# Three more kinds of edit to a fp32r transformer block: output stage 10 of 16 groups by seven, second down block 16 of 22, up stage's side stream eight steps sooner

## The chip, the cores and the metric

The kernel runs on one core of one Trainium2 chip. The metric is the device time of one execution in microseconds (us). A profile of one execution shows what each engine did: TensorE (PE) multiplies, VectorE (DVE) adds and subtracts, ScalarE (ACT) casts and applies functions, SyncE (SP) issues nearly all DMAs, GpSimd (POOL) does little here.

## The reference, cut to what matters

One transformer block for 256 tokens of width 2048 in float32. Three attention branches are gated and merged, the output projection is added to the residual, and a feed-forward part with a depthwise convolution of width 3 follows. The change touches the two products with `w_out` (2048 x 2048) and `w_down` (5632 x 2048), and work that goes on beside the product with `w_up`.

```python
def reference(x, mem, ...):
    ...
    merged = (g[:, :, 0] * (o_fox @ w_br_fox[l])
              + g[:, :, 1] * (o_sb @ w_br_sb[l])
              + g[:, :, 2] * (o_mem @ w_br_mem[l]))
    x = x + merged @ w_out[l]

    h2 = rms_norm(x, g_ffn[l])
    u = causal_depthwise_conv(h2 @ w_up[l], conv_w[l], conv_b[l])
    u_gate, u_val = jnp.split(u, 2, axis=-1)
    x = x + (jax.nn.silu(u_gate) * u_val) @ w_down[l]
```

## The kernel before, in words

**Precision.** Weights arrive from DRAM as float32 tiles of 128 x 1024 (`raw_*`). ACT casts a tile to the matmul's type (`hi_*`), DVE subtracts the cast from the tile (`lo_*`, "split" in what follows), and one product is three matmuls: activation hi x weight hi, activation lo x weight hi, activation hi x weight lo (`three`, L328 to L330 in the profile). The hi tiles have four buffers and so have the lo tiles (SBUFS = 4); a cast or a split that wants a fifth waits until PE has used the oldest. Raw tiles have four buffers of their own and, in the later stages, two more in turn (`raw_tile`).

**Blocks and groups.** The output product and the down product are computed by `blocked` (L367), each in two blocks of 1024 output columns. A block goes through pairs of k tiles (256 rows of the weights). One pair is a group, and a letter of the block's plan says how it is computed:

- `e`, by eight: 2 k tiles x 2 token tiles x 2 column halves = 8 products, 24 matmuls of 128x128 by 128x512. Two raw tiles are loaded (1.05 MB), cast and split.
- `s`, by seven: the 2 x 2 block product with seven products instead of eight, 21 matmuls. It needs four sums of the weights' quarters (T1 to T4) and three sums of the activations' (FS2 to FS4, and FS1). In the output and down stages the weight sums are made long before, and kept in DRAM; the group then loads 1.05 MB of sums beside 0.79 MB of weights, 1.835 MB in all. DVE splits three tiles of 1024 columns and one of 512.
- `f`, no matmuls: `form` makes the activation sums of one further pair (`pair_sums`, L334 to L346: DVE adds, ACT casts, DVE splits) for the down stage.

The gate stage (`name == "g"`) has a third form, `seven_here`: no sums are kept, DVE makes the four sums there from the raw tiles, into two further tiles (L440 to L443).

**Making sums ahead.** `halves` is one queue of (stage, block, pair, half) for all groups by seven that want kept sums, the output stage's first. Streams take from it beside other stages: each takes a group, loads its weights into a staging tile (`pre_*`), makes three DVE adds in place (`sums_in`, L247 to L251) and stores the sums to DRAM (`kept_*`). The last stream runs in the up stage (L1143): it begins after DU steps of that stage and takes a group every eight steps. A step is a call of `tick`, one per raw tile of the up stage.

**What sets the order.** Tile schedules instructions onto each engine's queue by priorities that follow from the program's order, except for those wrapped in `in_order`, which keep the order in which they are written. `ordered[0]` says whether `three` wraps its matmuls so. On each queue instructions then run in that order, and one that waits holds those behind it.

**After the last group by seven** of a block, `gather` adds its four banks into the residual on DVE. At the block's end four (in the last block five) adds follow and the output is stored.

Of the kernel before, what the change touches and what calls it, by code (L numbers as in the profile page):

```python
# [35 lines left out]
BLOCKS = 14  # L36
GS = 3
PF = 6
DU = 22


@with_exitstack
def hybrid_block(
# [25 lines left out]
    nc = tc.nc  # L69
# [28 lines left out]
    def later(gen):  # L98
        waiting.append(gen)
# [103 lines left out]
    def k_tiles(name):  # L203
# [19 lines left out]

    o_plans = ("eessesse", "eessesse")
    g_plans = (("", "esesesee", "esesesee"), ("esesesee", "esesesee", "esesesee"))
    d_plans = (
        "efefefef" + "sef" * 4 + "ssefsfssfssee",
        "efefef" + "sss" + "esss" * 3 + "ssee",  # L230
    )
    T1, T3, T4, T2 = range(4)
    FS2, FS4, FS3, FS1 = range(4)
    in_order = tc.keep_in_program_order
    dram = ctx.enter_context(tc.tile_pool(name="dram", bufs=1, space=bass.MemoryType.DRAM))
    by_k = lambda w: w[0].rearrange("(k p) n -> p k n", p=P)
    sums_of = {}
    ordered = [False]
    halves = deque(
        (name, by_k(w), nb, pr, h)  # L240
        for name, w, plans in (("o", w_out, o_plans), ("d", w_down, d_plans))
        for nb, plan in enumerate(plans)
        for pr in range(plan.count("s"))
        for h in range(2)
    )

# [120 lines left out]
    def blocked(name, w, nb, n0, plan, pair, sums, raw_tile, t4_tile, gathered, ready=None, form=None, apart=None):  # L367
# [4 lines left out]
        ns = plan.count("s")  # L372

        def a_of(p, j, t):
            v = pair(p, j)
# [83 lines left out]
            three(Y[1], *f_of(p, FS2), T2w, first, last)  # L459
            go_on()  # L460

        by_seven = seven_here if name == "g" else seven
        ahead = {}
        s, e = 0, ns
        for i, c in enumerate(plan):
            if c == "s":
# [4 lines left out]
                by_seven(s, s == 0, s == ns - 1)  # L471
                s += 1
                if s == ns:
                    later(gathered(n0, Y))
            elif c == "f":
                form()
            else:
                eight(e, i == 0, i == len(plan) - 1)
# [130 lines left out]
    def block(name, dt=F32):  # L609
        return bp.tile([P, 1024], dt, tag="blk", name=name)  # L610
# [384 lines left out]

    def merged_sums():
        yield 1
        for p in range(o_plans[0].count("s")):
            ms[p] = block(f"ms_{p}", F32R).rearrange("p (f l q) -> p f l q", f=4, l=2)
            pair_sums(mT[p], block(f"mw_{p}"), [(ms[p], slice(0, 4))])  # L1000
            yield 3

    raw_g = lambda name: wp.tile([P, PIECE], F32, tag="raw", name=name)

# [113 lines left out]

    raw_o = lambda name: raw_tile(name, lambda name: gp.tile([P, PIECE], F32, tag="pre", bufs=1, name=name))
    t4_o = (junk, lambda name: block(name)[:, :512])  # L1120
    for nb, plan in enumerate(o_plans):
        X = blocked(
            "o", w_out, nb, nb * PIECE, plan, lambda p, j: mT[p][:, j], lambda p, f: ms[p][:, f], raw_o, t4_o[nb],
            lambda n0, Y: gather(n0, Y, block),
        )
        for n in range(2):
            for t in range(NT):
                o = xres[:, t, nb * PIECE + n * 512 : nb * PIECE + (n + 1) * 512]
                nc.vector.tensor_tensor(o, o, X[t][n], ALU.add)
            later(hidden_T(2 * nb + n))  # L1130
# [120 lines left out]
        return dn[0].tile(shape, dt, tag=tag, name=name)  # L1251

    ov = out[0].rearrange("(t p) d -> p t d", p=P)
    N0, N1 = (plan.count("s") for plan in d_plans)
    sf = xt_pool.tile([P, 28, 2, P], F32R, tag="xt", name="sf")
    sf_more, sf_rest = [], []
    assert N0 == 11
# [3 lines left out]
    def s_of(p, f):  # L1261


        if f == FS1:
            return a_blocks[:, 2 * p, :, 1]
        if p < 9:
            return sf[:, 3 * p + f]
        if p == 9:
            return sf_more[0][:, f] if f < 2 else sf_rest[2]
        if p == 10:  # L1270
            return sf[:, 27] if f == 0 else sf_rest[f - 1]
        return a_blocks[:, 2 * (p - N0 + N1) + f // 2, :, f % 2]

    tmp_d = lambda name: place([P, PIECE], F32, "ts", name)

# [66 lines left out]
```

## Time and profile before

| | us |
|---|---|
| median of 3 runs | 1461.56 (1461.46 to 1463.46) |
| profiled execution | 1461.49 |
| its span | 1459.8 |
| PE busy in it | 1454.0 |
| DVE busy | 1213.4 |
| ACT busy | 850.0 |
| matmuls of the output blocks | from 658.8 to 743.0 |
| matmuls of the up stage | from 743.2 |
| first matmul of the down blocks | 1233.1 |

A row of a timeline reads: start, duration, engine, line, operation, tile written <- tiles read, shape, and in brackets how long the engine had stood idle before and what it waited for. A row with x2 or more is several such instructions in a row, without a long gap. A row of a group (line engine op out<-in xcount) has total busy time, the mean of one in ns, and the idle time before them. Matmuls overlap in the pipeline, so that the step from one start to the next is shorter than the duration of one.

### The profile page before, as it was taken

To read this page: it belongs to the slowest core of one execution; us is meant where nothing else is said; L and a number is where in the kernel's file an instruction comes from. 1 tells how busy PE (TensorE), PEld (TensorE's weight loads), DVE (VectorE), ACT (ScalarE), POOL (GpSimd) and SP (SyncE) were. 2 spreads that over 40 slices of the span, in tenths; PEclk is the share of its full clock that TensorE was granted. 3 is DMA by queue.
4 is the path that set the end of the run, shared out by engine and by line. 5 is a ranking of instruction groups with operands and counts; after the bars stand their busy time and mean duration, and the time that the engine had idled before them with its cause. 6 is when DMAs were issued, how large, how long until landed. Compare 5 with 4: busy or idle time off the path is not lost.

```text
span 1459.8 us, 20547 instructions
## 1 busy us (share of the span) xinstructions
PE 1454.0 (100%) x7314; PEld 1230.1 (84%) x7314; DVE 1213.4 (83%) x1791; ACT 850.0 (58%) x1212; POOL 19.3 (1%) x48
## 2 busy tenths in 40 slices
PE   9999999999999999999999999999999999999998
PEld 7888888888888888888888888888888888888887
DVE  5778777776898899997887888888888877999878
ACT  6755454564564555545666556556556565676665
POOL 0000000010000000000000000000000000000000
PEclk9999999999999999999999999999999999999999
DMA  9697798777668576788877888888888866899995
GB/s 312 202 330 248 267 341 288 238 241 222 209 207 269 172 231 198 270 265 263 276 196 232 288 266 306 278 273 299 283 281 298 267 200 202 253 291 333 299 324 222
DMA packets 162534, 381.08 MB, mean 261 GB/s; under 512 B 12234, under 2 KB 27486, under 8 KB 158334
## 3 DMA queue, kind: packets, MB, share of 16 engines
q1 hardware_dynamic: 161022, 377.52, 78.9%
q10 hardware_dynamic: 1328, 2.11, 0.4%
q8 instruction: 57, 0.93, 0.3%
q14 instruction: 47, 0.39, 0.1%
q0 software_dynamic: 80, 0.13, 0.0%
HBM read 343.01 MB, written 36.70 MB: 260 GB/s over the span
## 4 chain that ended last, share of the span: by engine, by line
PE 97%; DVE 1%; DMA 1%; issue 0%; SPq 0%; ACT 0%; DVEq 0%; ACTq 0%
PE u L1231 22%; PE u L1232 11%; PE xd L329 3%; PE xd L330 3%; PE xd L328 3%; PE xg L330 3%; PE xg L329 3%; PE xg L328 3%; PE s L328 2%; PE s L330 2%; PE f L330 2%; PE f L328 2%; PE f L329 2%; PE s L329 2%; PE b L330 2%; PE b L328 2%
## 5 line engine op out<-in xcount | busy, mean ns | idle before, releaser
L1231 PE MATMUL u<-hT,hi_u 128*128 128x512 f32 x1232 | 428.3, 394 | 0.0
L1232 PE MATMUL u<-hT,lo_u 128*128 128x256 f32 x1232 | 341.3, 277 | 0.0
L1231 PEld LDWEIGHTS u<-hT,hi_u 128*128 128x128 f32 x1232 | 231.0, 188 | 53.8
L143 DVE TENSOR_TENSOR lo_u<-raw_u,hi_u 128x1024 fp32r<-128x1024 f32 x176 | 215.1, 1222 | 73.2 <-ACT hi_u L142 71.9
L142 ACT CAST hi_u<-raw_u 128x1024 fp32r<-128x1024 f32 x176 | 184.7, 1050 | 135.0 <-PE u L1231 106.7
L1232 PEld LDWEIGHTS u<-hT,lo_u 128*128 128x128 f32 x1232 | 231.2, 188 | 0.0
L323 DVE TENSOR_TENSOR lo_d<-raw_d,hi_d 128x1024 fp32r<-128x1024 f32 x88 | 106.7, 1222 | 16.2 <-ACT hi_d L322 13.8
L322 ACT CAST hi_d<-raw_d 128x1024 fp32r<-128x1024 f32 x88 | 91.7, 1053 | 38.8 <-PE xd L329 17.8
L322 ACT CAST hi_g<-raw_g 128x1024 fp32r<-128x1024 f32 (+1 forms) x80 | 77.1, 972 | 48.9 <-PE xg L329 19.2
L323 DVE TENSOR_TENSOR lo_g<-raw_g,hi_g 128x1024 fp32r<-128x1024 f32 (+1 forms) x80 | 88.6, 1119 | 4.1 <-ACT hi_g L322 4.1
L142 ACT CAST hi_f<-raw_f 128x1024 fp32r<-128x1024 f32 (+1 forms) x40 | 38.5, 967 | 51.8 <-PE f L329 42.8
L330 PE MATMUL xg<-lo_g,xT 128*128 128x512 f32 x175 | 68.1, 389 | 0.0
L329 PE MATMUL xg<-hi_g,xT 128*128 128x512 f32 x175 | 68.1, 389 | 0.0
L328 PE MATMUL xg<-hi_g,xT 128*128 128x512 f32 x175 | 68.1, 389 | 0.0
L143 DVE TENSOR_TENSOR lo_f<-raw_f,hi_f 128x1024 fp32r<-128x1024 f32 (+1 forms) x40 | 44.6, 1118 | 22.3 <-ACT hi_f L142 21.7
L143 DVE TENSOR_TENSOR lo_s<-raw_s,hi_s 128x1024 fp32r<-128x1024 f32 (+1 forms) x40 | 44.7, 1117 | 20.9 <-ACT hi_s L142 20.9
L1231 PE MATMUL u<-hT_rest,hi_u 128*128 128x512 f32 x176 | 62.0, 394 | 0.0
L142 ACT CAST hi_b<-raw_b 128x1024 fp32r<-128x1024 f32 x32 | 33.6, 1051 | 45.2 <-DMA raw_b<-in_w_br_fox_dram 15.8
L142 ACT CAST hi_s<-raw_s 128x1024 fp32r<-128x1024 f32 (+1 forms) x40 | 38.4, 961 | 36.8 <-PE s L329 23.9
L1182 ACT ACTIVATE y<-u,taps 128x256 f32<-128x256 f32 x88 | 49.6, 596 | 16.3 <-DVE u L1177 16.2
L330 PE MATMUL xd<-lo_d,aT 128*128 128x512 f32 x148 | 57.6, 389 | 0.0
L328 PE MATMUL xd<-hi_d,aT 128*128 128x512 f32 x148 | 57.6, 389 | 0.0
(520 smaller groups left out, 3473.1 us busy)
## 6 DMA issues: line engine op xcount, KB each, us to landing
raw_u<-in_w_up_dram SPq DMA_DIRECT2D x176, 512.0 KB, 4.5
raw_g<-in_w_in_dram SPq DMA_DIRECT2D x96, 512.0 KB, 4.4
raw_d<-in_w_down_dram SPq DMA_DIRECT2D x63, 512.0 KB, 5.4
pre_d<-in_w_down_dram SPq DMA_DIRECT2D x17, 1024.0 KB, 6.2
kept_d<-pre_d SPq DMA_DIRECT2D x17, 1024.0 KB, 6.2
raw_f<-in_w_in_dram SPq DMA_DIRECT2D x32, 512.0 KB, 4.9
raw_s<-in_w_in_dram SPq DMA_DIRECT2D x32, 512.0 KB, 5.2
raw_t_d<-kept_d SPq DMA_DIRECT2D x25, 512.0 KB, 5.8
```

Source lines behind the costliest of these rows:

```text
L142: pin(nc.scalar.copy(hi[:, :m], raw[:, :m]))
L143: pin(nc.vector.tensor_tensor(lo[:, :m], raw[:, :m], hi[:, :m].bitcast(F32), ALU.subtract))
L322: nc.scalar.copy(hi[:, :n], src)
L323: nc.vector.tensor_tensor(lo[:, :n], src, hi[:, :n].bitcast(F32), ALU.subtract)
L328: fix(nc.tensor.matmul(o, lhsT=ah, rhs=w[0], start=first, stop=False))
L329: fix(nc.tensor.matmul(o, lhsT=al, rhs=w[0], start=False, stop=False))
L330: fix(nc.tensor.matmul(o, lhsT=ah, rhs=w[1], start=False, stop=last))
L1182: nc.scalar.activation(y, u[:, 2:], AF.Identity, scale=tap(2), bias=tap(3))
L1231: nc.tensor.matmul(ps[i], lhsT=hi[:, j, c], rhs=hT(k + j), start=first, stop=False)
L1232: nc.tensor.matmul(ps[i][:, :S], lhsT=lo[:, j, c], rhs=hT(k + j)[:, :S], start=False, stop=last)
```

## The change

- **Output stage.** Both blocks' plans go from four groups by seven of eight (`eessesse`) to five (`eessssse`), ten of sixteen in all. The pairs by seven are 0, 1, 2, 3 and 6 (`o_sevens`). Pair 6's activation sums are made by a new generator, `last_merged_sums`, which is queued right ahead of the output blocks and writes to a tile of the pool `op`. One more group per block has its weight sums kept in DRAM.
- **Second down block.** 16 groups by seven of 22 instead of 14. Thirteen are as before; the other three (`i`, pairs 2, 8 and 13) are computed by a new `seven_over`: it loads the pair's two raw tiles only, casts and splits the first product's half tile, and makes the four weight sums with four DVE adds of 128x512 in the raw tiles themselves, each after the cast and split of what it overwrites. Then the raw tiles, now holding sums, are cast and split again as T1, T3 and T4, T2. Two more `form`s make the activation sums of pairs 14 and 15; pair 15's go to slots of `sf` that pair 0 has used. All matmuls of this block keep the written order.
- **Up stage.** DU goes from 22 to 14, and the stream there takes 18 groups instead of 17. 34 groups have kept sums instead of 33 (10 of the output stage and 24 of the down stage, before 8 and 25).

By count the program has 12 matmuls less, 41 TENSOR_TENSOR and 3 SCALAR_TENSOR_TENSOR more on DVE, 17 casts more on ACT and 5 DMAs more on SP.

```diff
-DU = 22
+DU = 14
...
-    o_plans = ("eessesse", "eessesse")
+    o_plans = ("eessssse", "eessssse")
...
-        "efefef" + "sss" + "esss" * 3 + "ssee",
+        "efssiefsssefssisseffssissee",
     )
+    sevens = lambda plan: [c for c in plan if c in "si"]
...
+    o_sevens = (0, 1, 2, 3, 6)
+    pairs = lambda name, n: o_sevens if name == "o" else range(n)
...
-        for pr in range(plan.count("s"))
+        for pr, c in zip(pairs(name, 16), sevens(plan))
+        if c == "s"
         for h in range(2)
...
+        def seven_over(p, first, last):
+            raw0, raw1 = load(2 * p), load(2 * p + 1)
+            b0, b1 = (w.rearrange("p (n c) -> p n c", n=2) for w in (raw0, raw1))
+            (B00,) = parts(raw0[:, :512], f"{name}{nb}_{2 * p}")
+            three(Y[0], *a_of(p, 0, 0), B00, first, last)
+            nc.vector.tensor_tensor(b0[:, 0], b0[:, 0], b0[:, 1], ALU.add)
+            nc.vector.tensor_tensor(b0[:, 1], b0[:, 1], b1[:, 1], ALU.add)
+            B10, B11 = parts(raw1, f"{name}{nb}_{2 * p + 1}")
+            three(X[0][0], *a_of(p, 1, 0), B10)
+            three(X[0][1], *f_of(p, FS4), B11)
+            nc.vector.tensor_tensor(b1[:, 1], b0[:, 0], b1[:, 1], ALU.add)
+            nc.vector.tensor_tensor(b1[:, 0], b1[:, 1], b1[:, 0], ALU.add)
+            go_on()
+            T1w, T3w = parts(raw0, f"t_{name}{nb}_{2 * p}")
+            three(Y[2], *f_of(p, FS1), T1w, first, last)
+            three(Y[3], *f_of(p, FS3), T3w, first, last)
+            T4w, T2w = parts(raw1, f"t_{name}{nb}_{2 * p + 1}")
+            three(X[1][0], *a_of(p, 1, 1), T4w)
+            three(Y[1], *f_of(p, FS2), T2w, first, last)
+            go_on()
...
-        for p in range(o_plans[0].count("s")):
+        for p in range(4):
...
+    def last_merged_sums():
+        yield 2
+        after = op.tile([P, KT, 2 * S], F32R, tag="ot", name="m_after")
+        ms[6] = after[:, 0:2].rearrange("p k c -> p (k c)").rearrange("p (f l q) -> p f l q", f=4, l=2)
+        pair_sums(mT[6], block("mw_6"), [(ms[6], slice(0, 4))])
...
+    later(last_merged_sums())
     for nb, plan in enumerate(o_plans):
...
-        return a_blocks[:, 2 * (p - N0 + N1) + f // 2, :, f % 2]
+        if p == 15:
+            return sf[:, f]
+        over = a_pair(p - N0 + N1).rearrange("p k (l t q) -> p k l t q", l=2, t=NT)
+        return over[:, f // 2, :, f % 2]
...
     for nb, plan in enumerate(d_plans):
         apart = [] if nb == 1 else None
+        ordered[0] = nb == 1
```

DVE in the second down block, around pair 8. `lo_d_16` and `lo_d_17` are the splits of the pair's two weight tiles, `lo_t_d_8` those of its loaded sums. Before:

```order
L323 TENSOR_TENSOR lo_t_d_7_13365<-raw_t_d_7_13340,hi_t_d_7_13364 128x1024
L323 TENSOR_TENSOR lo_t_d_7_13375<-raw_t_d_7_13342,hi_t_d_7_13374 128x512
L323 TENSOR_TENSOR lo_d_16_13391<-raw_d_16_13381,hi_d_16_13390 128x1024
L323 TENSOR_TENSOR lo_d_17_13401<-raw_d_17_13384,hi_d_17_13400 128x1024
L323 TENSOR_TENSOR lo_t_d_8_13411<-raw_t_d_8_13386,hi_t_d_8_13410 128x1024
L323 TENSOR_TENSOR lo_t_d_8_13421<-raw_t_d_8_13388,hi_t_d_8_13420 128x512
```

After the change (L327 is the line of the split, L471, L472, L476 and L477 are the four adds, `lo_t_d_16` and `lo_t_d_17` the splits of the sums in the raw tiles):

```order
L327 TENSOR_TENSOR lo_t_d_7_13337<-raw_t_d_7_13304,hi_t_d_7_13336 128x512
L327 TENSOR_TENSOR lo_d_16_13348<-raw_d_16_13343,hi_d_16_13347 128x512
L471 TENSOR_TENSOR raw_d_16_13343<-raw_d_16_13343 128x512
L472 TENSOR_TENSOR raw_d_16_13343<-raw_d_16_13343,raw_d_17_13345 128x512
L327 TENSOR_TENSOR lo_d_17_13357<-raw_d_17_13345,hi_d_17_13356 128x1024
L327 TENSOR_TENSOR lo_t_d_16_13369<-raw_d_16_13343,hi_t_d_16_13368 128x1024
L476 TENSOR_TENSOR raw_d_17_13345<-raw_d_16_13343,raw_d_17_13345 128x512
L477 TENSOR_TENSOR raw_d_17_13345<-raw_d_17_13345 128x512
L327 TENSOR_TENSOR lo_t_d_17_13379<-raw_d_17_13345,hi_t_d_17_13378 128x1024
L327 TENSOR_TENSOR lo_d_18_13398<-raw_d_18_13388,hi_d_18_13397 128x1024
```

The splits of two loaded sum tiles have gone. In their place stand four adds and two splits of whole tiles; the second pair of adds stands behind the split of the first buffer's sums, and the last split behind both.

DVE around pair 13, after the change, and ahead of it the coefficient sums of pair 15 (`fw_13529`):

```order
L350 TENSOR_TENSOR aT<-fw_13529,aT 128x128
L327 TENSOR_TENSOR lo_d_25_13608<-raw_d_25_13591,hi_d_25_13607 128x1024
L327 TENSOR_TENSOR lo_t_d_12_13618<-raw_t_d_12_13593,hi_t_d_12_13617 128x1024
L327 TENSOR_TENSOR lo_t_d_12_13628<-raw_t_d_12_13595,hi_t_d_12_13627 128x512
L327 TENSOR_TENSOR lo_d_26_13639<-raw_d_26_13634,hi_d_26_13638 128x512
L471 TENSOR_TENSOR raw_d_26_13634<-raw_d_26_13634 128x512
L327 TENSOR_TENSOR lo_d_27_13648<-raw_d_27_13636,hi_d_27_13647 128x1024
L472 TENSOR_TENSOR raw_d_26_13634<-raw_d_26_13634,raw_d_27_13636 128x512
L476 TENSOR_TENSOR raw_d_27_13636<-raw_d_26_13634,raw_d_27_13636 128x512
L477 TENSOR_TENSOR raw_d_27_13636<-raw_d_27_13636 128x512
L327 TENSOR_TENSOR lo_t_d_26_13660<-raw_d_26_13634,hi_t_d_26_13659 128x1024
L327 TENSOR_TENSOR lo_t_d_27_13670<-raw_d_27_13636,hi_t_d_27_13669 128x1024
```

Here three adds stand together behind the split `lo_d_27`, ahead of both splits of sums. Before the change there is no form at this place.

DVE in the early part of the up stage (`lo_u_1_14` is the stage's eighth split of its second half, `lo_u_0_0` the next tile's). Before:

```order
L1184 SCALAR_TENSOR_TENSOR y_0_6994<-u_6990,taps,y_0_6994 128x256
L143 TENSOR_TENSOR lo_u_1_14_7145<-raw_u_1_14_7143,hi_u_1_14_7144 128x1024
L1177 TENSOR_TENSOR u_6992<-y_0_6997,rbc 128x256
L1183 SCALAR_TENSOR_TENSOR y_0_6997<-u_6992,taps,y_0_6997 128x256
L1184 SCALAR_TENSOR_TENSOR y_0_6997<-u_6992,taps,y_0_6997 128x256
L143 TENSOR_TENSOR lo_u_0_0_7176<-raw_u_0_0_7174,hi_u_0_0_7175 128x1024
L1177 TENSOR_TENSOR u_6990<-y_0_7022,rbc 128x256
L143 TENSOR_TENSOR lo_u_0_2_7203<-raw_u_0_2_7201,hi_u_0_2_7202 128x1024
```

After, where L253 to L255 are the three adds of the stream's first group (`pre_d_6`):

```order
L1218 SCALAR_TENSOR_TENSOR y_0_7022<-u_7018,taps,y_0_7022 128x256
L143 TENSOR_TENSOR lo_u_1_14_7176<-raw_u_1_14_7174,hi_u_1_14_7175 128x1024
L253 TENSOR_TENSOR pre_d_6_7167<-pre_d_6_7167 128x1024
L254 TENSOR_TENSOR pre_d_6_7167<-pre_d_6_7167 128x512
L143 TENSOR_TENSOR lo_u_0_0_7210<-raw_u_0_0_7208,hi_u_0_0_7209 128x1024
L255 TENSOR_TENSOR pre_d_6_7167<-pre_d_6_7167 128x512
L1211 TENSOR_TENSOR u_7020<-y_0_7025,rbc 128x256
L1211 TENSOR_TENSOR u_7018<-y_0_7050,rbc 128x256
```

The stream's adds stand between the splits there; before, the first of them came later. On SP the load of that staging tile now stands ahead of the loads of `raw_u_1_14` and what follows:

```order
L141 DMA raw_u_1_10_7122<-in_w_up_dram 128x2x512
L141 DMA raw_u_1_12_7144<-in_w_up_dram 128x2x512
L305 DMA pre_d_6_7167<-in_w_down_dram 128x2x1024
L141 DMA raw_u_1_14_7174<-in_w_up_dram 128x2x512
L141 DMA raw_u_0_0_7208<-in_w_up_dram 128x2x512
L141 DMA raw_u_0_2_7235<-in_w_up_dram 128x2x512
```

Before the change, SP went from one tile of the stage to the next at this place.

More of the change, by code (lines that the diff above doesn't have):

```diff
@@ L371, in blocked @@
         Y = []
-        ns = plan.count("s")
+        ns = len(sevens(plan))
         def a_of(p, j, t):
@@ L460, in seven_here @@
             go_on()
-        by_seven = seven_here if name == "g" else seven
+        def seven_over(p, first, last):
[18 more added lines that the diff above has]
+            go_on()
+        by_seven = {"s": seven_here if name == "g" else seven, "i": seven_over}
         ahead = {}
-        s, e = 0, ns
+        s, e = 0, 0
+        sp = pairs(name, ns)
+        ep = [p for p in range(len(plan) - plan.count("f")) if p not in sp]
         for i, c in enumerate(plan):
-            if c == "s":
+            if c in "si":
                 if s == 0:
@@ L470, in blocked @@
                     Y += [bank(f"y{name}{nb}_{j}") for j in range(4)]
-                by_seven(s, s == 0, s == ns - 1)
+                by_seven[c](sp[s], s == 0, s == ns - 1)
                 s += 1
@@ L477, in blocked @@
             else:
-                eight(e, i == 0, i == len(plan) - 1)
+                eight(ep[e], i == 0, i == len(plan) - 1)
                 e += 1
@@ L1253, in hybrid_block @@
     ov = out[0].rearrange("(t p) d -> p t d", p=P)
-    N0, N1 = (plan.count("s") for plan in d_plans)
+    N0, N1 = (len(sevens(plan)) for plan in d_plans)
     sf = xt_pool.tile([P, 28, 2, P], F32R, tag="xt", name="sf")
```

## The prediction

> **What bounds the kernel now.** I read the page's busy shares first, then the chain that ended last, then PE's timeline for the price of one matmul.
>
> ```profile
> PE 1454.0 (100%) x7314; PEld 1230.1 (84%) x7314; DVE 1213.4 (83%) x1791; ACT 850.0 (58%) x1212; POOL 19.3 (1%) x48
> PE 97%; DVE 1%; DMA 1%; issue 0%; SPq 0%; ACT 0%; DVEq 0%; ACTq 0%
> ```
>
> TensorE is busy nearly all of the span of 1459.8 us and carries 97% of the chain. So time falls only with fewer matmuls, and rises only where PE has to wait. A wait anywhere else counts once it has used up the lead with which weights are ready ahead of PE.
>
> ```profile
> 1362.18 0.39 PE L330 MATMUL yd<-lo_d,aT 128*128 128x512 f32 x1
> 1366.94 0.39 PE L330 MATMUL yd<-lo_d,aT 128*128 128x512 f32 x1
> ```
>
> These are the same matmul of two neighbouring groups by seven in the last block: 21 matmuls in 4.76 us, so one costs 4.76/21 = 0.227 us. The 0.39 us in the rows is its length in the pipeline, part of which lies over the next matmul. A group by eight has 24, so 5.44 us.
>
> **What is removed.** One group in each output block and two in the second down block go from 24 matmuls to 21: 4 x 3 = 12 matmuls x 0.227 us = 2.72 us, all on PE and so all on the path, if nothing new waits. The time cannot fall by more; it is 0.19% of it. A measurement of this kernel tells about 0.2%, 2.9 us, from no change. The Trainium skill (TensorE: Matmul & The Clock Gate, section Back-to-back issue gap) gives about 131 ns per matmul of 512 columns in a sustained stream; by that estimate the saving would be 1.57 us and the result 1.15 us later. The rows above say 227 ns, and the measurement decides.
>
> **The three groups over their own buffers.** In the second down block three groups by seven make their weight sums on DVE in the raw buffers, between the splits of their own weights. Rows of DVE, ACT and PE where pair 8 is computed before the change:
>
> ```profile
> 1406.31 1.83 DVE L323 TENSOR_TENSOR lo_t_d<-raw_t_d,hi_t_d 128x1024 fp32r<-128x1024 f32 x2
> 1408.35 2.58 DVE L323 TENSOR_TENSOR lo_d<-raw_d,hi_d 128x1024 fp32r<-128x1024 f32 x2 [0.21 <-ACT hi_d L322]
> 1411.07 1.83 DVE L323 TENSOR_TENSOR lo_t_d<-raw_t_d,hi_t_d 128x1024 fp32r<-128x1024 f32 x2
> 1407.26 1.06 ACT L322 CAST hi_d<-raw_d 128x1024 fp32r<-128x1024 f32 x1 [0.47 <-PE yd L329]
> 1410.69 0.39 PE L328 MATMUL yd<-hi_d,aT 128*128 128x512 f32 x1
> 1411.14 0.39 PE L330 MATMUL yd<-lo_d,aT 128*128 128x512 f32 x1
> ```
>
> PE begins the group at 1410.69 and needs its first lo tile at 1411.14. DVE finished that tile about 1.57 us earlier (1408.35 plus the 1.22 of one split, below), and in a run of sevens this lead is all there is: the cast waits for PE to free a hi buffer (0.47), so nobody runs further ahead. In each such group DVE makes three splits of 1024 columns and one of 512, some 4.0 us by the durations below, in 4.76 us.
>
> Sums of that kind stand in the trace in the gate stage:
>
> ```profile
> 405.25 0.69 DVE L441 TENSOR_TENSOR t_g<-raw_g,raw_g 128x512 f32<-128x512 f32 x1
> 405.85 0.69 DVE L442 TENSOR_TENSOR t_g<-t_g,raw_g 128x512 f32<-128x512 f32 x1
> 407.66 1.22 DVE L323 TENSOR_TENSOR lo_g<-raw_g,hi_g 128x1024 fp32r<-128x1024 f32 x1
> 408.79 2.36 DVE L323 TENSOR_TENSOR lo_t_g<-t_g,hi_t_g 128x1024 fp32r<-128x1024 f32 x2
> ```
>
> An add of 128x512 takes 0.60 us up to the next independent instruction and 0.69 to its end; a split of 1024 columns 1.13 (408.79 - 407.66) and 1.22. The new group has four adds (2.4 to 2.8 us), a split of 512 columns (0.6) and three of 1024 (3.4 to 3.7): about 6.5 us of DVE against 4.76 of PE. The lead of 1.57 nearly covers the excess of 1.75. What it does not cover is the end of the chain: the last cast on ACT needs the last add and the last split needs that cast, and meanwhile DVE idles.
>
> Walk for pair 8, zero at PE's first matmul, DVE in the order shown in the text before: split 16 from -2.64 (its cast of 512 columns is the shorter), add 1 ends at -1.23, add 2 at -0.51, split 17 runs from -0.60 to 0.62. ACT casts the first buffer's sums from -0.46 to 0.59 (1.06, as in the row), DVE splits them from 0.63 to 1.85. Add 3 ends at 2.45, add 4 at 3.18. ACT casts the second buffer's sums from 3.22 to 4.27. PE's sixteenth matmul, due at 15 x 0.227 = 3.40, reads that cast: it waits 0.91 us. Its split runs from 4.31 to 5.53, and PE's eighteenth, now due at 3.40 + 0.91 + 0.45 = 4.76, waits 0.81. Together 1.72 us. Behind this group the splits come just in time, and each seven wins back 4.76 - 4.0 = 0.74 us of lead.
>
> Pair 2 has the same chain, with three small instructions of a coefficient sum between its splits and adds. Their rows:
>
> ```profile
> L337 DVE TENSOR_TENSOR fw<-aT 128x512 f32<-128x512 f32 x14 | 9.6, 688 | 0.2
> L340 DVE TENSOR_TENSOR fw<-fw 128x256 f32<-128x256 f32 x14 | 5.9, 419 | 0.1
> L341 DVE SCALAR_TENSOR_TENSOR fw<-fw 128x128 f32<-128x128 f32 x14 | 4.1, 290 | 0.3
> L342 DVE TENSOR_TENSOR fw<-fw 128x128 f32<-128x128 f32 x14 | 4.0, 288 | 0.1
> L346 DVE TENSOR_TENSOR aT<-fw,aT 128x128 fp32r<-128x128 f32 x23 | 5.8, 285 | 0.0
> ```
>
> They are 0.29 + 0.29 + 0.28 = 0.86 us at most, so the group costs from 1.7 (all in idle time) to 2.6 (all on the chain); 2.0, because one of them falls where DVE would otherwise wait for ACT. Pair 13 has both later adds ahead of the split of the first sums; the same walk gives 0.7. But the added coefficient sums of pairs 14 and 15 lie ahead of it, some 3.7 us of them (0.69 + 0.42, two of 0.29, seven of 0.28) within two groups of seven that have 1.5 us to spare: 2.2 us of lead go, more than the 1.57 of a run of sevens. With nothing left pair 13 pays 0.7 + 1.57 = 2.3. The group by eight before them lets DVE get further ahead, as each of its tiles lasts PE 2.72 us; I take 1.5, the middle.
>
> The last wait of the trace shows what starting again costs:
>
> ```profile
> 421.76 0.39 PE L329 MATMUL xg<-hi_t_g,xT 128*128 128x512 f32 x1
> 422.28 0.50 PE L330 MATMUL xg<-lo_t_g,xT 128*128 128x512 f32 x1
> 422.62 0.40 PE L328 MATMUL yg<-hi_t_g,xs 128*128 128x512 f32 x1
> ```
>
> The wait is 0.52 - 0.227 = 0.29 us, and the matmul after it also comes 0.34 - 0.227 = 0.11 late. For six waits that is between 0 and 0.66; I take 0.33, since the two of a group lie close.
>
> **The other parts.** Rows of engine load and DMA by window (PE, PEld, DVE, ACT, POOL, granted clock, DMA share, GB/s):
>
> ```profile
> 680.00:700.00 20.00, 20.00 (x90) 16.57 (x89) 16.48 (x18) 12.63 (x14) 0.00 (x0) 1.00 0.91 298
> 780.00:800.00 20.00, 20.00 (x117) 17.51 (x116) 18.59 (x36) 16.39 (x26) 0.00 (x0) 1.00 0.82 263
> 1320.00:1340.00 20.00, 20.00 (x90) 16.54 (x89) 18.64 (x20) 14.13 (x17) 0.00 (x0) 1.00 0.99 363
> 1400.00:1420.00 20.00, 20.00 (x90) 16.53 (x89) 15.57 (x15) 13.27 (x14) 0.00 (x0) 1.00 0.98 341
> ```
>
> Down block 2's weights: a seven from kept sums loads 1.835 MB, the other two kinds 1.05. Before 14 x 1.835 + 8 x 1.05 = 34.1 MB, now 13 x 1.835 + 9 x 1.05 = 33.3: no more than at 1400, where PE does not wait. Taken at 0, between -0.1 (nothing waits there to be won) and +0.5 (one late load).
>
> Output blocks: each eight made a seven adds 4.0 - 2.3 = 1.7 us to DVE, where the 680 window leaves it 3.5 in 20. Sums of the coefficients (2.4 us) come before the stage's sevens. Five sevens in a row ask for 1.835 MB per 4.76 us, 385 GB/s, above any window; at the 363 of the row at 1320 a group takes 5.05 us, 0.29 short each, 1.45 per block. The stage has such waits for DMA already, hidden by leads of some us:
>
> ```profile
> ACT hi_o L322 <- DMA raw_o<-kept_o: 3.2, 1, 3.2
> ```
>
> I take 0, bounds 0 and 2.9: the run is five groups long, and the loads of four raw buffers stand ahead of it.
>
> Up stage: 18 groups of weight sums instead of 17, begun eight steps sooner, so that the first load (1 MB) and its three adds (about 2.4 us, one of 1024 columns and two of 512) fall in its early part, from about 780 on. There ACT has just waited for late weights:
>
> ```profile
> 774.40 2.06 ACT L142 CAST hi_u<-raw_u 128x1024 fp32r<-128x1024 f32 x2 [5.73 <-DMA raw_u<-in_w_up_dram]
> 775.48 2.36 DVE L143 TENSOR_TENSOR lo_u<-raw_u,hi_u 128x1024 fp32r<-128x1024 f32 x2 [5.49 <-ACT hi_u L142]
> 778.50 1.23 DVE L143 TENSOR_TENSOR lo_u<-raw_u,hi_u 128x1024 fp32r<-128x1024 f32 x1 [0.66 <-PE u L1232]
> 778.55 0.27 PE L1232 MATMUL u<-hT,lo_u 128*128 128x256 f32 x1
> ```
>
> The first of the two lo tiles is ready at 776.70 and used at 778.55, a lead of 1.85 us. At 778.50 DVE already waits again for PE to free a buffer (0.66), so it is as far ahead as the buffers let it before the adds come. So 0, with 0.6 as the other end (2.4 - 1.85). The new order of the sums in the gate stage moves which group is summed, not how many per step: 0.
>
> **The sum.** -2.72 + 1.72 + 2.0 + 1.5 + 0.33 = +2.83 on the profiled execution's 1461.49 us (span 1459.8 and 1.7 around it, 0.07 below the median of the runs): 1464.3 us. The bounds of the three groups alone, 1.7 + 1.7 + 0.7 and 1.8 + 2.6 + 2.3 with 0 to 0.66, give +1.4 to +4.6; the likeliest case's own range is 1462.9 to 1466.0.
>
> **Rivals.**
> - The three groups are hidden (other side). If DVE and ACT enter each with 1.7 us more lead than 1.57, PE never waits: -2.72, 1458.8 us. For it speaks that all work of a group but the last cast and split could run early; against it the ring of four buffers (ACT's 0.47 on PE). Half hidden, with 0.9 us per group: 1461.5.
> - The output stage becomes DMA-bound: +1.5 to +2.9 beside the forecast, 1465.8 to 1467.2. It decides once the buffers loaded ahead are spent before the fifth group. For it: share 0.91 already at 298 GB/s; against: fast windows of 363. The Trainium skill (DMA: Bandwidth & Descriptors, section Where 436 GB/s comes from) sets the HBM side at about 358 GB/s per core. By that estimate a group would take 5.13 us and the ten 3.7 us more than PE; the window at 363 agrees with the figure to 2%, and buffers ahead would have to carry the rest.
> - The earlier stream meets those late weights of the up stage: +0.6 to +2 (its 1 MB also delays the next 0.5 MB load by 1.05/363 = 2.9 us, against a lead of 1.85), about 1465.6. It decides if the load at 775 is pushed back.
>
> **How the numbers follow.** Forecast 0.60; half or more hidden, 1460 to 1462.9, 0.16; wholly hidden 0.05; output stage 0.12; up stage 0.07. The range 1461.2 to 1466.8 leaves out the wholly hidden case, the lowest of the partly hidden and the top of the output stage's. Slower by over 0.2% begins at 1464.5, just above my time: a little under half of the forecast's 0.60, 0.28, and nearly all of the last two, 0.18, make 0.46. Faster by over 0.2% needs more than can be removed: 0.03 for the whole gain plus the noise of a run. The rest, 0.51, is no change that can be told.
>
> **What would show it.** In the profile after: PE's chain has 12 matmuls less; DVE's four adds in each new group with ACT's cast waiting behind the last; PE idle twice in each of three groups, 0.7 to 0.9 each; no wait of PE between 422 us and the second down block. Wrong if PE is idle in the output or up stage, if the new groups pass without waits, or if DVE's adds on a buffer in place take other than 0.6 to 0.7 us.

## The result and the profile after

The changed kernel takes 1465.92 us (median of 21 runs, 1463.78 to 1475.44), the kernel before in the same comparison 1461.65 (21 runs, 1461.16 to 1463.46). The ratio is 1.0033 with a 95% interval of 1.0023 to 1.0042: slower, by 4.3 us between the medians. 1464.3 was predicted, with 1461.2 to 1466.8 as the range. The profiled execution of the changed kernel took 1465.78 us, with a span of 1464.1.

The busy shares and the chain of the changed kernel:

```profile
PE 1455.0 (99%) x7302; PEld 1228.5 (84%) x7302; DVE 1234.7 (84%) x1835; ACT 857.6 (59%) x1229; POOL 19.0 (1%) x48
PE 96%; DVE 2%; DMA 1%; issue 1%; ACT 0%; SPq 0%; DVEq 0%; ACTq 0%
```

PE has 12 instructions less (7302 for 7314), and its share of the chain falls by a point; DVE and "issue" gain (the shares are rounded). All waits of PE from 600 us to the end (engine, line, waited for: us in total, times, longest); before the change the same view has no row:

```profile
PE xd L332 <- ACT hi_t_d L326: 1.5, 2, 1.0
PE xd L334 <- DVE lo_t_d L327: 1.1, 2, 0.5
PE yd L334 <- DVE lo_t_d L327: 1.0, 2, 0.7
```

All of them lie in the three new groups. Their cost is not the waits alone, but each step from one matmul to the next beyond 0.227 us. Pair 8 on PE, with what the eye should look at, the starts:

```profile
1405.37 0.39 PE L334 MATMUL yd<-lo_t_d,sf 128*128 128x512 f32 x1
1406.71 0.50 PE L332 MATMUL xd<-hi_t_d,aT 128*128 128x512 f32 x1 [0.95 <-ACT hi_t_d L326]
1407.05 0.39 PE L333 MATMUL xd<-hi_t_d,aT 128*128 128x512 f32 x1
1407.97 0.50 PE L334 MATMUL xd<-lo_t_d,aT 128*128 128x512 f32 x1 [0.53 <-DVE lo_t_d L327]
1408.31 0.40 PE L332 MATMUL yd<-hi_t_d,sf 128*128 128x512 f32 x1
```

1.34 - 0.227 = 1.11 us before the sixteenth matmul, 0.92 - 0.227 = 0.69 before the eighteenth, and 0.11 after each of the two: 2.03 us. DVE and ACT meanwhile:

```profile
1400.33 0.69 DVE L471 TENSOR_TENSOR raw_d<-raw_d 128x512 f32<-128x512 f32 x1
1401.05 0.69 DVE L472 TENSOR_TENSOR raw_d<-raw_d,raw_d 128x512 f32<-128x512 f32 x1
1401.66 1.22 DVE L327 TENSOR_TENSOR lo_d<-raw_d,hi_d 128x1024 fp32r<-128x1024 f32 x1
1402.95 1.23 DVE L327 TENSOR_TENSOR lo_t_d<-raw_d,hi_t_d 128x1024 fp32r<-128x1024 f32 x1
1404.09 0.69 DVE L476 TENSOR_TENSOR raw_d<-raw_d,raw_d 128x512 f32<-128x512 f32 x1
1404.81 0.69 DVE L477 TENSOR_TENSOR raw_d<-raw_d 128x512 f32<-128x512 f32 x1
1406.69 1.23 DVE L327 TENSOR_TENSOR lo_t_d<-raw_d,hi_t_d 128x1024 fp32r<-128x1024 f32 x1 [1.19 <-ACT hi_t_d L326]
1405.61 1.04 ACT L326 CAST hi_t_d<-raw_d 128x1024 fp32r<-128x1024 f32 x1 [2.70 <-PE yd L333]
```

The last add ends at 1405.50, ACT casts at 1405.61 (the row blames PE, but the last event before it is DVE's add), and DVE stands idle 1.19 us for that cast, with PE waiting for both. These times lie within 0.2 us of the prediction's walk for pair 8, counted from PE's first matmul of the group at 1402.20: the second cast of sums at 3.42 to 4.46 (walk 3.22 to 4.27), its split at 4.49 to 5.72 (4.31 to 5.53).

The other two groups lose their time a little differently:

```profile
1363.46 0.50 PE L334 MATMUL yd<-lo_t_d,aT 128*128 128x512 f32 x1 [0.29 <-DVE lo_t_d L327]
...
1437.06 0.50 PE L334 MATMUL yd<-lo_t_d,aT 128*128 128x512 f32 x1 [0.69 <-DVE lo_t_d L327]
```

Pair 2 has the two waits of pair 8 (0.71 and 0.69) and ahead of them one of 0.45 at 1363.46, for the split of its first sums; 2.20 us with what comes late behind each. Pair 13 has one wait, 0.86 at 1437.06, for the split that stands on DVE behind three adds; 1.13 us in all. There DVE is not idle; its queue is late.

Where the time went, by stage (from the starts of the first matmuls of each stage, in us):

| | before | after | after, second profile (e1_again) |
|---|---|---|---|
| start, up to the first fox matmul | 81.06 | 82.67 | 81.05 |
| from there to the output blocks | 577.78 | 577.67 | 577.77 |
| output blocks | 84.36 | 83.00 | 83.43 |
| up stage | 489.95 | 489.95 | 489.95 |
| down blocks and the end | 226.63 | 230.78 | 230.76 |
| span | 1459.8 | 1464.1 | 1463.0 |

The down blocks cost 4.15 us: 5.36 in the three groups less 1.36 for six matmuls (the rest, 0.15, is in steps too small to name). The output blocks give their 1.36 in the first profile and 0.93 in the second. The remaining 1.6 us of the first profile lie in the start, where both programs issue the same DMAs.

### The profile page after: what moved, and what is told of

The parts are those of the page before. It is cut to its first block, busy times and chain, and to the rows that moved or that the text cites. A ratio compares the mean times of both kernels' runs of the same rounds, so it can differ in the third digit from the quotient of the medians.

```text
span 1464.1 us, 20615 instructions
## 1 busy us (share of the span) xinstructions
PE 1455.0 (99%) x7302; PEld 1228.5 (84%) x7302; DVE 1234.7 (84%) x1835; ACT 857.6 (59%) x1229; POOL 19.0 (1%) x48
## 4 chain that ended last, share of the span: by engine, by line
PE 96%; DVE 2%; DMA 1%; issue 1%; ACT 0%; SPq 0%; DVEq 0%; ACTq 0%
PE u L1265 22%; PE u L1266 11%; PE xd L334 3%; PE xg L334 3%; PE xd L333 3%; PE xd L332 3%; PE xg L333 3%; PE xg L332 3%; PE s L332 2%; PE s L334 2%; PE f L334 2%; PE f L332 2%; PE f L333 2%; PE s L333 2%; PE b L333 2%; PE b L334 2%
## 5 line engine op out<-in xcount | busy, mean ns | idle before, releaser
L327 DVE TENSOR_TENSOR lo_d<-raw_d,hi_d 128x1024 fp32r<-128x1024 f32 (+1 forms) x88 | 104.6, 1202 | 9.4 <-ACT hi_d L326 7.9
L326 ACT CAST hi_d<-raw_d 128x1024 fp32r<-128x1024 f32 (+1 forms) x88 | 89.9, 1038 | 36.7 <-PE xd L333 14.2
L327 DVE TENSOR_TENSOR lo_g<-raw_g,hi_g 128x1024 fp32r<-128x1024 f32 (+1 forms) x80 | 88.7, 1120 | 4.3 <-ACT hi_g L326 4.3
L332 PE MATMUL s<-hi_s,xT 128*128 128x512 f32 (+1 forms) x140 | 54.1, 386 | 0.0
L326 ACT CAST hi_t_g<-t_g 128x1024 fp32r<-128x1024 f32 x30 | 31.5, 1051 | 38.2 <-PE xg L333 36.5
```

The costliest lines, as they stand in the source:

```text
L326: nc.scalar.copy(hi[:, :n], src)
L327: nc.vector.tensor_tensor(lo[:, :n], src, hi[:, :n].bitcast(F32), ALU.subtract)
L332: fix(nc.tensor.matmul(o, lhsT=ah, rhs=w[0], start=first, stop=False))
```

## The experiments

Medians in us; "before" is the kernel before, measured beside it on the same chip.

| run | median (lowest to highest, runs) | before | ratio, 95% interval |
|---|---|---|---|
| e1_again | 1465.65 (1464.14 to 1473.72, 11) | 1461.65 | 1.003, 1.0019 to 1.0041 |
| e2_no_adds | 1460.15 (1458.34 to 1462.06, 11) | 1461.65 | 0.9988, 0.9979 to 0.9996 |
| e3_i_to_e | 1462.71 (1461.25 to 1471.10, 12) | 1461.65 | 1.0014, 1.0000 to 1.0027 |
| e4_e_then_i | 1459.94 (1458.90 to 1470.62, 12) | 1461.65 | 0.9997, 0.9981 to 1.0013 |
| e5_d_alone | 1461.75 (1460.44 to 1464.67, 11) | 1461.89 | 0.9999, 0.9991 to 1.0008 |
| e6_o_alone | 1463.96 (1461.58 to 1472.01, 12) | 1461.89 | 1.0025, 1.0009 to 1.0041 |
| e7_stream_sooner | 1461.70 (1461.05 to 1462.80, 11) | 1461.89 | 0.9997, 0.9988 to 1.0006 |
| e8_before_again | 1462.04 (1461.34 to 1464.36, 11) | 1461.89 | 1.0002, 0.9993 to 1.0010 |
| e9_o_again | 1464.79 (1 run) | 1462.65 | |
| e10_e_then_i_sooner | 1471.43 (1461.99 to 1473.24, 12) | 1462.65 | 1.0045, 1.0028 to 1.0061 |
| e11_sooner_hT_later | 1468.44 (1462.96 to 1474.18, 12) | 1461.94 | 1.0045, 1.0028 to 1.0062 |
| e12_e_then_i_hT_later | 1461.14 (1460.24 to 1462.88, 11) | 1461.94 | 0.9997, 0.9988 to 1.0005 |

**e1_again** has no edit.

> The changed kernel as it is, once more. The profile of it showed 5.36 us of waits of PE in the three new groups (2.20, 2.03 and 1.13) less 2.72 us of matmuls, and 1.6 us more in the first 80 us (the first fox-projection matmul at 82.67 against 81.06 before), where both programs issue the same DMAs. Theory A (the start varies from execution to execution, the three groups do not): waits of 5.2 to 5.5 us in the three groups again, and the first fox matmul anywhere from 81 to 84. Theory B (the changed program itself starts later): that matmul again within 0.3 of 82.67. Time 1464 to 1467.5 by both.

The three groups lost 5.37 us by the same count (5.36 before); the first fox matmul came at 81.05 instead of 82.67. Both profiles agree on the groups' price and differ in the start: theory A.

**e2_no_adds** leaves out the adds.

```diff
-            nc.vector.tensor_tensor(b0[:, 0], b0[:, 0], b0[:, 1], ALU.add)
-            nc.vector.tensor_tensor(b0[:, 1], b0[:, 1], b1[:, 1], ALU.add)
...
-            nc.vector.tensor_tensor(b1[:, 1], b0[:, 0], b1[:, 1], ALU.add)
-            nc.vector.tensor_tensor(b1[:, 0], b1[:, 1], b1[:, 0], ALU.add)
```

> The four adds of the three new groups are left out (so the weight sums of these groups are not formed); loads, casts, splits and matmuls stay. Theory (the chain of adds, cast and split makes PE wait): no wait of PE over 0.2 us in the second down block, time 5.4 us below the changed kernel, 1460.5 by the medians. Rival (loads or the ring of raw and hi buffers make it wait, the two raw buffers of such a group being held over two casts): 2 us of waits or more stay, 1462.5 to 1464.

5.5 us less than e1_again, and no wait of PE after 600 us. Loads, casts and splits are the same in number, so those alone do not make PE wait; the twelve adds do, which together occupy DVE for 12 x 0.69 = 8.3 us. This edit takes out two things at once, DVE's time for the adds and the order that they impose on the second casts; the next run keeps both and gives DVE more lead.

**e4_e_then_i** moves the three groups.

```diff
-        "efssiefsssefssisseffssissee",
+        "efssseifssseifssseiffssssee",
```

> The changed kernel with each new group standing right behind a group by eight (plan efsss eifsss eifsss eiffssss ee), everything else kept, so that DVE has the 3.2 us that a group by eight leaves it, and the hi and lo rings hold tiles that PE uses for 2.72 us each. Theory (a matter of lead: DVE needs 6.5 us in 4.76, with 1.7 us more lead nothing waits): no wait of PE over 0.2 us in the block, 5.4 us below the changed kernel, 1460.5, and 1 to 2.7 us below the kernel before. Rival (the order of adds, cast and split in the group costs PE its wait whatever the lead): 0.7 to 1.7 us of wait in each of the three, 1463 to 1466.

5.7 us less than e1_again, with all twelve adds in place. DVE in the first of the moved groups (e4_e_then_i):

```profile
1365.30 0.69 DVE L471 TENSOR_TENSOR raw_d<-raw_d 128x512 f32<-128x512 f32 x1
1365.91 1.22 DVE L327 TENSOR_TENSOR lo_d<-raw_d,hi_d 128x1024 fp32r<-128x1024 f32 x1
1367.05 0.69 DVE L472 TENSOR_TENSOR raw_d<-raw_d,raw_d 128x512 f32<-128x512 f32 x1
1367.65 0.28 DVE L350 TENSOR_TENSOR aT<-fw,aT 128x128 fp32r<-128x128 f32 x1
1367.85 0.68 DVE L476 TENSOR_TENSOR raw_d<-raw_d,raw_d 128x512 f32<-128x512 f32 x1
1368.45 0.28 DVE L350 TENSOR_TENSOR aT<-fw,aT 128x128 fp32r<-128x128 f32 x1
1368.65 0.68 DVE L477 TENSOR_TENSOR raw_d<-raw_d 128x512 f32<-128x512 f32 x1
1369.26 1.22 DVE L327 TENSOR_TENSOR lo_t_d<-raw_d,hi_t_d 128x1024 fp32r<-128x1024 f32 x1
1370.39 0.28 DVE L350 TENSOR_TENSOR aT<-fw,aT 128x128 fp32r<-128x128 f32 x1
1370.71 0.69 DVE L341 TENSOR_TENSOR fw<-aT 128x512 f32<-128x512 f32 x1
1371.32 1.22 DVE L327 TENSOR_TENSOR lo_t_d<-raw_d,hi_t_d 128x1024 fp32r<-128x1024 f32 x1
```

DVE does not idle here: the time before the last split goes to coefficient sums (L350, L341). From the first add to the end of the last split the chain takes 7.2 us, for pair 8 of the changed kernel it took 7.6; what changed is that DVE enters it earlier. The first add starts 4.4 to 4.6 us ahead of PE's first matmul of the group in the three groups, against 1.6 to 1.9 in the changed kernel, and the last split ends at 2.7 to 2.8 us after it, where PE needs it at 3.85. Moving a group also changed which pairs are computed so and the order of DVE's instructions, but that order, but for the coefficient sums between, is the one that pair 13 had in the changed kernel, where it cost 1.13 us. So the order alone does not make the wait. The rival, a wait whatever the lead, falls. PE's only wait after 600 us is then in the output stage:

```profile
PE hT L196 <- DVE xres_again L1163: 0.5, 1, 0.5
```

**e3_i_to_e** keeps the output and up stages and takes the three groups out.

```diff
-        "efssiefsssefssisseffssissee",
+        "efsseefsssessessessessee",
```

> The three new groups become groups by eight and the three coefficient sums of pairs 13 to 15 go; output and up stage as changed. Against the kernel before: 6 matmuls less in the output blocks, 3 more in the second down block, 3 x 0.227 = 0.7 us less. Theory (output and up stage cost nothing but their matmuls): no wait of PE after 560 us, 0.7 us faster than before, 1461.0. Rival (output stage or up stage loses time on DMA): 1462 to 1464, with a wait of PE between 660 and 800.

1.06 us above the kernel before, not 0.7 below. Its profile has one wait after 600 us, 0.3 us, at the same transposes in the output stage, for DVE's add and not for DMA; its start was a late one (82.99). **e5_d_alone** is the other half:

```diff
-DU = 14
+DU = 22
...
-    o_plans = ("eessssse", "eessssse")
+    o_plans = ("eessesse", "eessesse")
...
-        "efssiefsssefssisseffssissee",
+        "efssseifssseifssseiffssssee",
...
-    o_sevens = (0, 1, 2, 3, 6)
+    o_sevens = (0, 1, 2, 3)
...
-    later(last_merged_sums())
```

> The second down block alone, with each new group behind a group by eight; output stage with four groups by seven per block, up stage's stream from step 22 as before. 6 matmuls less, 1.36 us. Theory (the rest of the measured time beyond the three groups' waits comes from the output stage and from the start): no wait of PE after 560 us, 1460.3 by the medians, the matmuls of the output blocks over in 84.4 us as before, no run near 1470. Rival (it comes from the second down block too): 1461 or more, and single runs about 10 us longer again.

In its profile the second down block gives exactly what it should (the down blocks' matmuls take 220.32 us from first to last, before 221.68), PE has no wait after 600 us, and no run was long. But the median is 0.14 us below the kernel before, not 1.36: the time is the rival's, the place is not. The profile shows a start of 81.83 (0.77 later), 0.57 us lost at one wait in the gate stage (381 us), and 5.52 us instead of 4.94 from the last matmul of `xd` to the end; none of these is in code that the edit touches. **e8_before_again**, the kernel before once more, has the first two:

> The kernel before, once more, for its start: in the profiles so far the first fox-projection matmul came at 81.05 to 81.34 in three and at 82.67 to 82.99 in three. If the start varies by itself, it is near 81 or near 83 here too, and the median is 1461.65 with a spread of 2 us upwards; if the changed programs start later, it is near 81.06.

Its first fox matmul came at 83.20, and it lost 0.76 us at 382. So these stages vary from one execution to the next, the kernel before included: over all fourteen profiles the start takes 81.05 to 83.20 us, the way from there to the output blocks 577.35 to 578.51, and the end 4.59 to 5.52. The first profile of the kernel before was one with an early start and without a wait in the gate stage. **e7_stream_sooner** moves only the up stage's stream in the kernel before.

```diff
-DU = 22
+DU = 14
```

> The kernel before with the up stage's stream eight steps sooner (17 groups) and nothing else. Theory (hidden): 1461.65, the up stage's matmuls over in 489.8 us as before, no wait of PE there. Rival (the stream's first load collides with the weights that were late at 774): 1462.3 or more with a wait of PE near 780, and single runs 10 us longer.

Nothing: 1461.70 beside 1461.89, the up stage's matmuls in 489.83 us. **e6_o_alone** takes the output stage alone; so that all 35 kept sums are made in time, its stream starts at step 6.

```diff
-DU = 14
+DU = 6
...
-        "efssiefsssefssisseffssissee",
+        "efefef" + "sss" + "esss" * 3 + "ssee",
```

> The output stage alone, with five groups by seven per block; the second down block as before. Since that needs 35 kept sums, the up stage's stream starts at step 6 and takes 19 groups. 6 matmuls less, 1.36 us. Theory (five groups by seven on end make DVE late for the transposes after the first block): PE waits 0.3 to 0.6 us in the transposes near 706, the output blocks take 83.3 to 83.7 us against 84.36 before, 1460.7 to 1461.3, and single runs 10 us longer again. Rival (that stage costs nothing): 83.0 us, 1460.3.

The output blocks took 83.35 us, as the theory had it, with a wait of 0.2 at their transposes. What it had not foreseen is the up stage, where PE waited as well, and a median 3 us higher. The waits between 745 and 900, and then PE, ACT and DVE at the first two and at the third:

```profile
PE u L1266 <- DVE lo_u L143: 1.6, 2, 0.8
PE u L1265 <- ACT hi_u L142: 0.7, 1, 0.7
```

```profile
790.24 0.51 PE L1265 MATMUL u<-hT,hi_u 128*128 128x512 f32 x1 [0.66 <-ACT hi_u L142]
791.50 0.39 PE L1266 MATMUL u<-hT,lo_u 128*128 128x256 f32 x1 [0.75 <-DVE lo_u L143]
789.14 1.05 ACT L142 CAST hi_u<-raw_u 128x1024 fp32r<-128x1024 f32 x1 [1.97 <-PE u L1265]
787.78 1.23 DVE L253 TENSOR_TENSOR pre_d<-pre_d 128x1024 f32<-128x1024 f32 x1 [1.07 <-DMA pre_d<-in_w_down_dram]
789.04 0.69 DVE L254 TENSOR_TENSOR pre_d<-pre_d 128x512 f32<-128x512 f32 x1
790.22 1.22 DVE L143 TENSOR_TENSOR lo_u<-raw_u,hi_u 128x1024 fp32r<-128x1024 f32 x1 [0.49 <-ACT hi_u L142]
```

```profile
815.21 0.39 PE L1266 MATMUL u<-hT,lo_u 128*128 128x256 f32 x1 [0.84 <-DVE lo_u L143]
813.01 0.68 DVE L255 TENSOR_TENSOR pre_d<-pre_d 128x512 f32<-128x512 f32 x1
813.61 0.42 DVE L1224 TENSOR_TENSOR y<-y,y 128x256 f32<-128x256 f32 x1
813.94 1.22 DVE L143 TENSOR_TENSOR lo_u<-raw_u,hi_u 128x1024 fp32r<-128x1024 f32 x1
```

Near 790 PE waits for ACT's cast and for the split of it, and DVE, done with two of the stream's adds at 789.73, itself stands idle 0.49 us for that cast. The cast is late; its row blames PE, but in e10 the row of the same cast names the load of its weights (1.48 us). The stream's 1 MB load is issued at 780.2, and the weight loads issued between 779 and 790 take 6.2 to 8.9 us to land, in the same window of the changed kernel 3.6 to 6.7. That is the third rival of the prediction, the stream's load in front of the weights, at a setting it was not meant for; that the load held the cast is read from these times and was not tried by itself. At 815 DVE is not idle: the stream's next three adds, from 810.54 on, stand ahead of the split that PE waits for. At step 14 neither occurred in any profile, at step 6 PE waited at both places in all.

**The long runs.** The kernel before never took more than 1464.6 us. The changed kernel took 1473.7 to 1475.4 in 3 of 32 runs, e3 and e4 some 1470 in 2 of 12 each, e6 in 4 of 12. **e9_o_again** (e6's program) and **e10_e_then_i_sooner** (e4 with `DU = 6`) were to catch one.

> The output stage alone, the same program as e6_o_alone, for a second look at the up stage's first 60 us: there PE waited 2.9 us between 786 and 815, DVE's adds of the stream (in fixed order) stood waiting for a load that came late, and four of its runs were some 9 us longer. If these two belong together, an execution with a time above 1469 shows a wait of PE of some 10 us between 745 and 830; one near 1463 shows 0 to 3 us there. If they don't, the time missing in a long execution stands in another stage.

> The kernel of e4_e_then_i (new groups behind groups by eight, output stage as changed) with the up stage's stream from step 6 instead of 14. Theory (the stream's early loads and adds meet the slow loads at 760 to 775): a wait of PE of 1 to 3 us between 745 and 830, median 1461 to 1463 against 1459.9, and more long runs, a third of them. Rival (DU has nothing to do with it): 1459.9 and one or two long runs of twelve.

e9's execution was an ordinary one (1464.79). e10 was long in 9 of 12 runs, more than its theory's third, with a median of 1471.43, so that its rival, by which `DU` does not matter, falls. Its profiled execution is a long one (span 1470.3), and there the expected wait of 10 us does not exist: PE's waits over 0.1 us in the whole up stage come to 1.8 us, yet its matmuls took 501.5 us instead of 489.85. PE's timeline near 1000 us in e4 (first) and in the long execution of e10, with pairs of one 512-column and one 256-column matmul, and the start three pairs on as the last row of each:

```profile
999.81 0.39 PE L1265 MATMUL u<-hT,hi_u 128*128 128x512 f32 x1
1000.04 0.28 PE L1266 MATMUL u<-hT,lo_u 128*128 128x256 f32 x1
1000.16 0.39 PE L1265 MATMUL u<-hT,hi_u 128*128 128x512 f32 x1
...
1000.85 0.39 PE L1265 MATMUL u<-hT,hi_u 128*128 128x512 f32 x1
```

```profile
1000.07 0.40 PE L1265 MATMUL u<-hT,hi_u 128*128 128x512 f32 x1
1000.31 0.28 PE L1266 MATMUL u<-hT,lo_u 128*128 128x256 f32 x1
1000.42 0.40 PE L1265 MATMUL u<-hT,hi_u 128*128 128x512 f32 x1
...
1001.13 0.40 PE L1265 MATMUL u<-hT,hi_u 128*128 128x512 f32 x1
```

Three pairs take 1.04 us in e4, 1.06 in e10; over 64 matmuls 11.09 and 11.31 us. The windows from 900 to 940 of e4 and e10 (PE, PEld, DVE, ACT, POOL, granted clock, DMA share, GB/s) show no difference beyond the fewer instructions that fit in: the granted clock is 1.00 of full speed in both, and PE never idle.

```profile
900.00:940.00 40.00, 40.00 (x233) 35.28 (x232) 35.33 (x59) 24.11 (x37) 0.00 (x0) 1.00 0.84 283
```

```profile
900.00:940.00 40.00, 40.00 (x228) 34.67 (x227) 33.23 (x56) 24.01 (x38) 0.00 (x0) 1.00 0.84 282
```

So in this long execution PE steps 2% slower through the up stage, from its start to its end but for some 10 us behind the wait at 791, where two pairs take 0.693 us as in e4 instead of 0.70 to 0.71; near 802.7 it falls back, with no wait there. The other long runs have no profile. In e6, e9 and e11 the slower step holds only for stretches between 785 and 815, and in all three it ends at a wait of 0.8 to 0.9 us at 815 to 816.5; a wait of 1.0 us at 815 in e10 did not end it. In e11 it sets in near 785.8 and again near 799, both times with no wait. So PE can leave the slower step at a wait; what brings PE into it these profiles do not show.

**e11_sooner_hT_later** and **e12_e_then_i_hT_later** were to tell whether the short wait at 706, which e10 has and the kernel before has not, is what starts it.

```diff
     def hidden_T(n):
-        yield
+        yield 3 if n < 2 else 0
```

> The kernel of e10_e_then_i_sooner with the transposes after the first output block two steps later (36 matmuls further back on PE), and nothing else. In the long execution of e10 the whole up stage ran at 11.31 us per 64 matmuls instead of 11.09 with the granted clock at 1.00 and hardly any wait: 9.4 us. Programs with a wait of PE at those transposes (0.2 to 0.6 us at 706) have long runs, those without (the kernel before, e2, e5, e7) had none. Theory A (that wait brings PE into the slower step): no wait at 706, the up stage at 11.09 from its start, at most two long runs of twelve (nine of twelve before), median 1461 to 1463. Theory B (the stream from step 6, with its waits near 790 and 814, or something else in the output stage does it): long runs stay the most, median 1470 or more.

> The kernel of e4_e_then_i (stream from step 14) with the transposes after the first output block two steps later. Theory A: no wait of PE after 560 us, 0.4 us less than e4, median 1459 to 1459.7, no run above 1465; then faster than both kernels. Theory B: long runs as in e4, two of twelve, and the median as there, 1459.9.

Neither settles it. The wait at 706 went, but PE now waited 1.57 us (e11) and 1.56 (e12) at 719, which the profiles put down to DVE's work on the transposed tiles; in e12:

```profile
PE yo L332 <- DVE hT L185: 1.4, 1, 1.4
```

e11 was long in 6 of 12 runs, e12 in none of 11 with the same wait. In the counts the start step of the stream stands out (19 of 36 long at step 6, e6, e10 and e11 together; 7 of 78 at step 14 with five groups by seven, the changed kernel included). With four groups by seven per output block no run was long; step 6 was not tried with them. What PE's step hangs on when the up stage begins stays open.

No kernel that computes all its sums was clearly faster than the one before (e2 was, by 0.1%, and leaves the sums out). e4 comes closest, ten of its twelve runs from 1458.90 to 1460.84, two near 1470.

## Why the prediction was right, point by point

- **12 matmuls at 0.227 us: right.** Output blocks 84.36 to 83.00 us, down block 1.36 by e5: 2.72 as said. Each of the two halves, six matmuls for 1.36 us, gives 227 ns. The 131 ns of the Trainium skill (TensorE: Matmul & The Clock Gate, section Back-to-back issue gap) would have made it 1.57; the trace does not agree.
- **The chain in the new groups: right in kind and in its sum.** Pair 8 was given 0.91 + 0.81 and had 1.11 + 0.69. Pair 2 was given 2.0 and had 1.86 beside its restarts, pair 13 1.5 and had 0.86: the coefficient sums ahead of it cost less lead than the middle of the bounds, and its price is near the 0.7 of the walk without them. The restarts were given 0.33 in all and took 0.78, 0.11 behind each of seven waits (one of them, in pair 13, of 0.05 only), so a restart is paid each time. Sum 5.55 against 5.36. That the sums agree so well is partly luck: pair 13 was given 0.64 too much, the restarts 0.45 too little. And the pattern was not the two waits in each group that the prediction asked for, but three, two and one, leaving out that short one.
- **Which of two things bound: lead, as argued.** The prediction said that the whole excess of DVE, 1.75 us per group, is nearly covered by the lead of 1.57, and that what remains uncovered is the cast and split at the end. That end of the chain is what pair 8 waited for; the waits of pair 13 and the first of pair 2 are DVE's own lateness, splits behind adds. e4 shows the side that the first rival named, more lead: with a group by eight ahead DVE enters 2.6 to 3.0 us earlier and the three groups cost nothing. Whether 1.7 us would have been enough, as the rival said, was not tried.
- **Output stage at 0: nearly.** Against 83.00 us nothing was lost in the first profile and in e2, and 0.43 to 0.67 us in e1, e3 and e4: a wait of PE where the prediction said none. It was not the rival's. No matmul of the groups by seven waited for DMA, which at 695 to 702 us of the first profile moved 384 GB/s, about what five groups by seven in a row ask for and more than any window that the prediction had. The transposes behind the block waited for DVE's residual adds. With the fifth group by seven DVE is busier there (11.0 of the 12 us from 683 to 695, before 8.7); that this is why the adds come late is read from the profile and not tested.
- **Up stage at 0: right at step 14** (e7, and 489.95 in both profiles of the changed kernel), except in the long runs, if these are long there as the one of e10 was. At step 6 it would have been wrong.
- **What was missed.** The profiled run of the kernel before was taken as the base, though start and gate stage vary by 2 and 1 us; and the long runs were not foreseen. The working gives +2.8; the second profile, with an early start, gives +3.2 in its span, the first +4.3, the medians +4.3 and +4.0. About 1 us of the medians is not traced to a stage. It is seen in e2, e3, e4 and e5 too, which were slower by 1.2, 1.7, 1.0 and 1.2 us than their counted matmuls say (the output stage holds 0.5 of e3's and 0.7 of e4's), and not in e7. The runs of the changed kernel are also spread more widely: their middle half covers 2.0 us, that of the kernel before 0.8. So the missing time may be a late start or a wait in the gate stage that comes more often, and not the same delay each time; one profile of each program can't tell.
- **The chances.** 0.46 had been given to slower by more than 0.2%, 0.51 to no telling change. The ratio's whole interval lies above 1.002, by the sum of the forecast and of these unforeseen 1 to 1.5 us.

## What to carry to other kernels

Where PE is the bound, work that makes its operands on the fly is free only if the helper engine's whole chain for the group, with the hand-overs to ACT and back, fits into PE's time for the group plus the lead at its start. Count that lead from the ring's size and the PE time per tile: the same kind of group cost 1.1 to 2.2 us behind a run of short groups and nothing behind one long group. A saving of 0.2% needs more profiles than one of either kernel, since stages that the edit does not touch moved by as much.

## What the runs showed of the hardware that was not expected

- The same alternating stream of 512- and 256-column matmuls ran at 11.09 or 11.31 us per 64 at a granted clock of 1.00 and without idle time. A wait of 0.8 to 0.9 us near 815 ended the slower step in e6, e9 and e11; in e10 it held for nearly the whole stage, 501.5 us instead of 489.85.
- After each wait in the three groups the matmul that follows the awaited one came another 0.11 us late. At the transposes of 128 columns it was 0.06 (0.165 instead of 0.109 in e4).
- An add of 128x512 that overwrites what the add before it reads started 0.72 us after it (1400.33 and 1401.05), and so did one that needs the result of the one before (1404.09 and 1404.81); an independent instruction started 0.61 after (1401.05 and 1401.66).
